# Two-layer hybrid attention network on one core: keys and queries projected ahead of the values, and one pair's keys ahead of the first scores

## The chip, the core and the metric

The kernel runs on one core of a Trainium2 chip. The metric is the device time of one execution in microseconds, the median of several runs. Five engines work side by side, each through its own list of instructions in a fixed order: TensorE (PE in the profile), VectorE (DVE), ScalarE (ACT), GpSimd (POOL) and SyncE (SP), which here only issues DMAs. An instruction that has to wait holds up everything behind it in its engine's list.

## The reference

The network has two layers, 512 tokens, a model width of 1024 and heads of 64. Layer 0 has 8 heads of attention with a decay ("fox"), and 8 heads of attention over the 128 highest-scoring keys of each query ("dsa"), where a small indexer gives the score. Layer 1 has 16 heads of plain causal attention in effect ("moba": with two blocks of 256, the own block and every earlier one are taken). Each layer ends with a gated convolution FFN. Cut to what the change touches:

```python
fq, fk, fv, ff, dq, ckv, dkr, iq, ik, iw = jnp.split(proj, split_points, axis=-1)
log_f = jax.nn.log_sigmoid(ff + b_fox_f)           # decay of each fox head
c = jnp.cumsum(log_f, axis=1)
s = einsum('bqhd,bkhd->bhqk', q_i, k) * scale + c_i - c_k   # fox scores, causal
p = softmax(s); out = einsum('bhqk,bkhd->bqhd', p, v)
score = einsum('bqh,bqhk->bqk', iw, relu(dots)) * idx_scale # indexer, then top_k
```

## The kernel before

All products are float32 made of two parts: each operand is split into a rounded high part (`_h`) and the rest (`_l`), and `mm3` (line 154) multiplies high by high, high by low and low by high. A weight chunk of 128x1024 (`chunk`, line 133) is loaded by SP into `raw`, ACT rounds it to `wh`, and POOL (in the fox and dsa part, where `lo_on_pool` holds) or DVE subtracts to `wl`. `raw`, `wh` and `wl` have three buffers each, so a chunk's `wh` waits until TensorE has done with the chunk three before it.

`proj` (line 160) multiplies one chunk with all tokens: 24 matmuls of 512 columns. A fox pair of heads needs keys (`ks`) and queries (`qs`), one chunk each; every second pair also brings the values of its group of four heads (`vals`, `v_group`, line 385): two chunks, 96 matmuls of 256 columns. Keys and queries are scaled, split and then copied between partitions by DMAs from SP (`stack_k`: six moves, `stack_q`: three), since the scores of the first head of a pair need the two parts of a query stacked.

The order of the program is that of a work list. `heads` (line 524) takes the pairs in turn: first all work numbered up to the pair, then for each of its two heads the scores and the softmax (`soft`), a share of the work of the next pair, and the mix of the head before (`mix`). In layer 0 the index scores of query blocks 1 to 3 (`index_scores`, line 605; names `ix`, `rl`, `tmask`) stand between the pieces of the first pair, and the selections (`select`, line 622) between those of later pairs: 16 rounds of MAX and MATCH_REPLACE on DVE for each block.

A fox score also needs the running sum of the decay, made by a chain of small steps on 32 partitions (lines 641 to 659; names `la`, `lm`, `lu`, `ck`): ACT takes the exponential and the logarithm, each behind a table load, DVE the steps between, ACT and DVE the copies to `ck`. ACT reaches the first relu of the index scores (`rl`) only behind the copies of `ck`.

A scheduler of the framework then sets the order on each engine at build time, from this program order and its own cost table; engines' lists can therefore differ from the order of the source by some instructions.

Of the kernel before, what the change touches and what calls it, by code (L numbers as in the profile page):

```python
# [71 lines left out]
def hybrid_kernel(ctx: ExitStack, tc: tile.TileContext, xT_d, pos_d, const_d, vec_d, w_d, out_d, idx):  # L72
# [60 lines left out]
    def chunk(name, cut=0):  # L133
        raw = wp.tile([P, 1024], F32, tag="raw", bufs=N_W, name=f"raw_{name}")
        wh = wp.tile([P, 1024], F32R, tag="wh", bufs=N_W, name=f"wh_{name}")
        wl = wp.tile([P, 1024], F32R, tag="wl", bufs=N_W, name=f"wl_{name}")
        if cut:
            for s in (slice(0, cut), slice(cut, 1024)):
                nc.sync.dma_start(raw[:, s], w_d[idx[name]][:, s])
                split(wh[:, s], wl[:, s], raw[:, s])  # L140
                if s.start == 0:
                    nc.sync.dma_start(xT[:, 1], xT_d[:, 1])
            return wh, wl
        nc.sync.dma_start(raw, w_d[idx[name]])
        A.copy(wh, raw)  # L145
        if lo_on_pool:
            for n in range(0, 1024, 256):
                t = slice(n, n + 256)
                G.tensor_tensor(wl[:, t], raw[:, t], wh[:, t].bitcast(F32), op=OP.subtract)
        else:  # L150
            V.tensor_tensor(wl, raw, wh.bitcast(F32), op=OP.subtract)
        return wh, wl
# [7 lines left out]
    def proj(name, w=None):  # L160
        wh, wl = w or chunk(name)
        o = ps("mm", f"mm_{name}")
        for k in range(KT):
            s = slice(k * P, k * P + P)
            mm3(o, wh[:, s], wl[:, s], xh[:, k], xl[:, k], k == 0, k == KT - 1)
        return o
# [61 lines left out]
    def scaled(o, nm):  # L228
        y = tmp(f"sc_{nm}")
        V.tensor_tensor(y, o, RB, op=OP.mult)  # L230
        return y
# [11 lines left out]
    def stack_q(y, nm):  # L243

        h, l = halves(y, nm)
        a = big(f"{nm}_a")
        move(a[LO], h[LO])
        move(a[HI], l[LO])
        move(l[LO], h[HI])
        return a, l  # L250

    def stack_k(y, nm, eng=V):

        out = []
        for n, t in zip("hl", halves(y, nm, eng)):
            b = big(f"{nm}_b{n}")
            move(b[LO], t[HI])
            move(b[HI], t[HI])
            move(t[HI], t[LO])
            out += [t, b]  # L260
        return out[0], out[1], out[2], out[3]
# [123 lines left out]
    def v_group(nm, late=None):  # L385

        v = vtile(nm)
        o = [ps("mm", f"mm_{nm}_{b}", (P, 2, 256)) for b in range(2)]
        for c in range(2):
            wh, wl = chunk(f"{nm}{c}")  # L390
            for k in range(4):
                for b in range(NB):
                    s = slice(b * P, b * P + P)
                    kk = 4 * c + k
                    ws = slice(k * 256, k * 256 + 256)
                    mm3(o[b // 2][:, b % 2], xh[:, kk, s], xl[:, kk, s], wh[:, ws], wl[:, ws],
                        kk == 0 and b % 2 == 0, kk == KT - 1 and b % 2 == 1)
            if c == 0 and late is not None:
                late()
        rcol = scale["col"]  # L400
        for b in range(NB):
            src = o[b // 2][:, b % 2].rearrange("p (h c) -> p h c", c=64)
            A.activation(v[:, b, :, 0], src, AF.Identity, scale=rcol[:, b:b + 1])
            V.scalar_tensor_tensor(v[:, b, :, 1], src, rcol[:, b:b + 1], v[:, b, :, 0].bitcast(F32), op0=OP.mult, op1=OP.subtract)
        return v

    def out_proj(nm, o, done=None, part=range(4)):

        for dp in part:
            wh, wl = chunk(f"{nm}{dp}")  # L410
            for e in range(2):
                d = 2 * dp + e
                acc = ps("mm", f"mm_{nm}_{d}")
                for k in range(4):
                    s = slice((4 * e + k) * P, (4 * e + k + 1) * P)
                    mm3(acc, wh[:, s], wl[:, s], o[k][0], o[k][1], k == 0, k == 3)
                V.tensor_tensor(xT[:, d], xT[:, d], acc, op=OP.add)
                if done is not None:
                    done(d)
# [141 lines left out]
    w = chunk("misc", 512)  # L561
# [8 lines left out]
    w = [chunk("iq0")]  # L570
# [34 lines left out]
    def index_scores(i):  # L605
        w = P * (i + 1)
        sc = tmask[i]
        qs = slice(i * P, i * P + P)
        for h in range(4):
            o = ps("S", f"ix{i}_{h}")  # L610
            scores(o[:, :w], iq[h // 2], (ikh, ikh, ikl, ikl), h % 2, qs, w)
            r = tmp(f"rl{i}_{h}")[:, :w]
            wh = iwT[:, i, h:h + 1]
            prev = sc if h else causal[i]
            A.activation(r, o[:, :w], AF.Relu)
            if i == 1:
                V.scalar_tensor_tensor(sc, r, wh, prev, op0=OP.mult, op1=OP.add)
            else:
                A.activation(r, r, AF.Copy, scale=wh)
                G.tensor_tensor(sc, r, prev, op=OP.add)  # L620
# [43 lines left out]
    def fox(p):  # L664
        def vals():
            values["f", p // 2] = v_group(f"fv{p // 2}_")

        def qs():
            c["q"] = stack_q(scaled(proj(f"fq{p}"), f"fq{p}"), f"fq{p}")

        def ks():
            c["k"] = stack_k(scaled(proj(f"fk{p}"), f"fk{p}"), f"fk{p}", G)

        c = {"nm": f"f{p}", "v": ("f", p // 2), "hv": 2 * (p % 2), "bias": causal, "out": fo, "lo": G,
             "decay": [(selr[:, P + h:P + h + 1], ck) for h in (2 * p, 2 * p + 1)]}
        return c, ([vals] if p % 2 == 0 else []) + [ks, qs]

    def dsa(p):
        def vals():
# [29 lines left out]
    pairs, work = [], []  # L709
    for n in range(8):  # L710
        c, w = (fox if n < 4 else dsa)(n % 4)
        pairs.append(c)
        if n == 0:
            w = [x for i, f in enumerate(w) for x in (f, lambda i=i: index_scores(i + 1))]
# [29 lines left out]
    def moba(p):  # L744
        def vals():
            values["m", p // 2] = v_group(f"mv{p // 2}_", moba_scale if p == 0 else None)

        def qs():
            c["q"] = stack_q(rope(proj(f"mq{p}"), f"mq{p}"), f"mq{p}")

        def ks():
            c["k"] = stack_k(rope(proj(f"mk{p}"), f"mk{p}"), f"mk{p}")

        c = {"nm": f"m{p}", "v": ("m", p // 2), "hv": 2 * (p % 2), "bias": causal, "out": mo[p // 4]}
        return c, ([vals] if p % 2 == 0 else []) + [ks, qs]

    pairs, work = [], []
    for n in range(8):
        c, w = moba(n)
        pairs.append(c)  # L760
        work += [(n, f) for f in w]
        if n == 7:
            work.append((7, lambda: out_proj("oo0_", mo[0], part=[0])))
    work += [(8, lambda m=m: out_proj("oo0_", mo[0], part=[m])) for m in range(1, 4)]
# [157 lines left out]
```

## Time and profile before

| | us |
|---|---|
| median of 3 runs | 1264.75 (1263.06 to 1265.96) |
| the profiled execution | 1264.17 |
| its span, first to last instruction | 1262.4 |
| TensorE busy | 1222.1 (97%) |
| VectorE busy | 811.6 (64%) |
| mean granted TensorE clock | 0.995 |

TensorE is busy nearly throughout, so its 40 us of idle time are what a reordering can win, beside what a lower clock costs. Most of it lies in the first 180 us, which hold the start, the fox pairs and the selections. The fox part runs from 44 to about 180 us, dsa and its projection to 265, the first FFN to 640, moba to about 890, and the second FFN to the end.

### The profile page before, as it was taken

How to read it: one execution, taken by the hardware profiler on the slowest of the kernel's cores; microseconds unless marked ns; L12 is line 12 of the kernel's file. 1: busy time of each engine (PE TensorE's matmuls, PEld its weight loads, DVE VectorE, ACT ScalarE, POOL GpSimd, SP SyncE). 2: the span in 40 equal slices, each digit the busy share in tenths (PEclk: the TensorE clock that was granted, in tenths of full speed). 3: DMA queues.
4: the chain of work that ended last, by engine and by line, in shares of the span. 5: the costliest groups of instructions: out<-in, count | busy, mean ns of one | idle time of the engine just before them, and what ended most of it. 6: DMA issues, size and time to landing. Idle time of an engine off the chain costs nothing.

```text
span 1262.4 us, 16801 instructions
## 1 busy us (share of the span) xinstructions
PE 1222.1 (97%) x5996; PEld 1019.0 (81%) x5996; DVE 811.6 (64%) x1489; ACT 557.1 (44%) x969; POOL 359.0 (28%) x394
## 2 busy tenths in 40 slices
PE   6889999999999999999999999999999999999997
PEld 4768777877888888888887888888878888888887
DVE  7889988675554455554666778787655555444555
ACT  5563667654333233333444556556433333332334
POOL 3675557542111111111213223232212111111110
PEclk9999999999999999999999999999999999999998
DMA  5333435122333333333325434332333332333231
GB/s 193 101 100 114 117 101 134 57 82 83 100 100 100 100 94 93 97 90 95 112 93 138 109 106 117 107 107 67 90 95 100 100 94 92 99 100 101 92 92 67
DMA packets 57379, 127.24 MB, mean 101 GB/s; under 512 B 7584, under 2 KB 21024, under 8 KB 57296
## 3 DMA queue, kind: packets, MB, share of 16 engines
q1 hardware_dynamic: 56368, 124.81, 33.5%
q10 hardware_dynamic: 864, 1.17, 0.3%
q8 instruction: 47, 0.77, 0.2%
q14 instruction: 36, 0.29, 0.1%
q0 software_dynamic: 64, 0.20, 0.0%
HBM read 104.13 MB, written 2.10 MB: 84 GB/s over the span
## 4 chain that ended last, share of the span: by engine, by line
PE 75%; DVE 11%; issue 5%; ACT 4%; DMA 2%; POOL 2%; SPq 0%; POOLq 0%; ACTq 0%; DVEq 0%
PE mm_u L157 6%; PE mm_u L156 6%; PE mm_g L157 6%; PE mm_u L158 6%; PE mm_d L157 6%; PE mm_g L158 6%; PE mm_g L156 6%; PE mm_d L158 6%; PE mm_d L156 6%; DVE tmask L627 2%; DVE m L626 1%; PE t_m L369 1%; PE o_m L378 1%; PE mm_mq L157 1%; PE mm_mq L156 1%
## 5 line engine op out<-in xcount | busy, mean ns | idle before, releaser
L431 POOL TENSOR_TENSOR cv<-cv,gs 128x512 f32<-128x512 f32 x44 | 57.1, 1297 | 550.0 <-ACT gs L430 550.0
L156 PE MATMUL mm_d<-a_h,wh_d 128*128 128x512 f32 (+1 forms) x384 | 143.1, 373 | 2.1 <-ACT a_h L128 2.1
L157 PE MATMUL mm_d<-a_l,wh_d 128*128 128x512 f32 (+1 forms) x384 | 142.9, 372 | 0.4 <-DVE a_l L129 0.4
L158 PE MATMUL mm_d<-a_h,wl_d 128*128 128x512 f32 (+1 forms) x384 | 142.7, 372 | 0.0
L500 DVE TENSOR_TENSOR us<-mm_u,cv 128x512 f32<-128x512 f32 x44 | 30.4, 692 | 168.1 <-PE mm_u L158 132.7
L157 PE MATMUL mm_g<-xl,wh_g 128*128 128x512 f32 x352 | 137.2, 390 | 0.4 <-DVE xl L172 0.4
L156 PE MATMUL mm_u<-xh,wh_u 128*128 128x512 f32 x352 | 137.4, 390 | 0.0
L158 PE MATMUL mm_u<-xh,wl_u 128*128 128x512 f32 x352 | 137.1, 389 | 0.0
L157 PE MATMUL mm_u<-xl,wh_u 128*128 128x512 f32 x352 | 137.1, 389 | 0.0
L156 PE MATMUL mm_g<-xh,wh_g 128*128 128x512 f32 x352 | 137.0, 389 | 0.0
L158 PE MATMUL mm_g<-xh,wl_g 128*128 128x512 f32 x352 | 137.0, 389 | 0.0
L145 ACT CAST wh_g<-raw_g 128x1024 fp32r<-128x1024 f32 x44 | 46.3, 1053 | 155.5 <-PE mm_g L157 153.9
L497 DVE TENSOR_TENSOR gs<-mm_g,RB 128x512 f32<-128x512 f32 x44 | 30.4, 691 | 121.9 <-PE mm_g L158 119.5
L128 ACT CAST wh_d<-raw_d 128x1024 fp32r<-128x1024 f32 x45 | 47.4, 1053 | 118.8 <-PE mm_u L157 107.3
L156 PEld LDWEIGHTS mm_d<-a_h,wh_d 128*128 128x128 f32 x384 | 72.4, 188 | 15.5 <-ACT a_h L128 3.0
L157 PEld LDWEIGHTS mm_d<-a_l,wh_d 128*128 128x128 f32 x384 | 72.4, 188 | 13.4 <-DVE a_l L129 1.1
L158 PEld LDWEIGHTS mm_d<-a_h,wl_d 128*128 128x128 f32 x384 | 72.4, 188 | 12.3
L157 PEld LDWEIGHTS mm_g<-xl,wh_g 128*128 128x128 f32 x352 | 66.1, 188 | 14.7 <-DVE xl L172 1.1
L156 PEld LDWEIGHTS mm_g<-xh,wh_g 128*128 128x128 f32 x352 | 66.1, 188 | 13.8
L156 PEld LDWEIGHTS mm_u<-xh,wh_u 128*128 128x128 f32 x352 | 66.1, 188 | 13.7
L158 PEld LDWEIGHTS mm_u<-xh,wl_u 128*128 128x128 f32 x352 | 66.1, 188 | 13.7
L158 PEld LDWEIGHTS mm_g<-xh,wl_g 128*128 128x128 f32 x352 | 66.1, 188 | 13.6
(778 smaller groups left out, 3074.1 us busy)
## 6 DMA issues: line engine op xcount, KB each, us to landing
raw_g<-in_w SPq DMA_DIRECT2D x44, 512.0 KB, 3.5
raw_u<-in_w SPq DMA_DIRECT2D x44, 512.0 KB, 3.6
raw_d<-in_w SPq DMA_DIRECT2D x41, 256.0 KB, 2.9
raw_d<-in_w SPq DMA_DIRECT2D x29, 192.0 KB, 2.6
raw_d<-in_w SPq DMA_DIRECT2D x34, 128.0 KB, 2.6
raw_oe<-in_w SPq DMA_DIRECT2D x8, 512.0 KB, 4.0
raw_mv<-in_w SPq DMA_DIRECT2D x8, 512.0 KB, 3.5
raw_mk<-in_w SPq DMA_DIRECT2D x8, 512.0 KB, 3.7
```

Of the source, the lines that this page charges most:

```text
L128: A.copy(dst_h, src)
L145: A.copy(wh, raw)
L156: PE.matmul(out, ah, bh, start=first, stop=False)
L157: PE.matmul(out, ah, bl, start=False, stop=False)
L158: PE.matmul(out, al, bh, start=False, stop=last)
L369: PE.transpose(t[:, n * P:n * P + P], probs[i][:, j * P:j * P + P], ident)
L378: PE.matmul(o[:, o0:o0 + w], vj, ph[:, c0:c0 + w], start=j == 0, stop=False)
L431: G.tensor_tensor(cv, cv, gs, op=OP.mult)
L497: V.tensor_tensor(gs, og, RB, op=OP.mult)
L500: V.tensor_tensor(us, ou, cv, op=OP.mult)
L626: V.max(m8, sc)
L627: V.match_replace(sc, m8, sc, -3e38)
```

## The change

In layer 0 each fox pair that brings values now projects keys and queries first and the values last. In layer 1 the keys of the second pair get the number of the first, so that they stand in front of the first pair's scores in the work list.

```diff
-        return c, ([vals] if p % 2 == 0 else []) + [ks, qs]
+        return c, [ks, qs] + ([vals] if p % 2 == 0 else [])
...
     for n in range(8):
         c, w = moba(n)
         pairs.append(c)
-        work += [(n, f) for f in w]
+
+        work += [(0 if n == 1 and f is w[0] else n, f) for f in w]
```

The index scores of the first pair keep their places in the list, one behind each piece: block 1 now comes behind the keys instead of the values, block 2 behind the queries, block 3 behind the values. Taken in order, the first four chunks after `ckv` were fv, fv, fk, fq and are now fk, fq, fv, fv.

On ACT, the stretch around the exponential and the logarithm of the decay (`la`, `lu`), with `ckv_h` the high part of the normalized latent keys, - before and + now:

```order
 L633 ACTIVATE sqkv<-sc_ckv 128x512
 L643 ACTIVATE la<-ry_misc,vec 32x512
+L145 CAST wh_fv_1_687<-raw_fv_1_686 128x1024
+L128 CAST ckv_h<-ckvn 128x512
 L645 ACT_TABLE_LOAD
 L645 ACTIVATE la<-la 32x512
-L128 CAST ckv_h<-ckvn 128x512
-L145 CAST wh_fq_708<-raw_fq_707 128x1024
 L648 ACT_TABLE_LOAD
 L648 ACTIVATE lu<-lu 32x512
```

The rounding of the fourth chunk moved from behind the exponential to in front of its table load; the chunk three before it is now fk.

On DVE, where the first fox scores (`s_f_0`, `s_f_1`) are read between the selection rounds of block 1 (`m_1_1306` is the first round, each next one is numbered 3 higher). Before:

```order
L627 MATCH_REPLACE tmask_91<-m_1_1345,tmask_91 128x256
L626 MAX m_1_1348<-tmask_91 128x8
L345 ISA prt_f_781,mx_f_0_786<-s_f_0_782,cmask 128x128
L345 ISA mx_f_0_786 128x1
L345 ISA prt_f_781,mx_f_1_793<-s_f_1_789,cmask 128x256
```

Now:

```order
L627 MATCH_REPLACE tmask_91<-m_1_1336,tmask_91 128x256
L345 ISA prt_f_781,mx_f_0_786<-s_f_0_782,cmask 128x128
L345 ISA mx_f_0_786 128x1
L626 MAX m_1_1339<-tmask_91 128x8
L345 ISA prt_f_781,mx_f_1_793<-s_f_1_789,cmask 128x256
```

Eleven rounds stand in front of the first score now, fourteen and a MAX did before.

On TensorE in layer 1, from the second head's third scores (`s_m_2` with `mk_bh`) through the transposes of the first head's probabilities (`t_m`). Before:

```order
L265 MATMUL s_m_2_6021<-mk_bh,mq_l 128x384
L266 MATMUL s_m_2_6021<-mk_bl,mq_l 128x384
L265 MATMUL s_m_3_6027<-mk_bh,mq_l 128x512
L266 MATMUL s_m_3_6027<-mk_bl,mq_l 128x512
L369 MATMUL t_m_0_6088<-const,prt_m_5928 128x128 x2
L369 MATMUL t_m_1_6095<-const,prt_m_5928 128x128
```

Now:

```order
L265 MATMUL s_m_2_6066<-mk_bh,mq_l 128x384
L266 MATMUL s_m_2_6066<-mk_bl,mq_l 128x384
L369 MATMUL t_m_0_6088<-const,prt_m_5977 128x128 x3
L369 MATMUL t_m_1_6095<-const,prt_m_5977 128x128 x2
L369 MATMUL t_m_0_6088<-const,prt_m_5977 128x128
L265 MATMUL s_m_3_6072<-mk_bh,mq_l 128x512
L266 MATMUL s_m_3_6072<-mk_bl,mq_l 128x512
L369 MATMUL t_m_1_6095<-const,prt_m_5977 128x128
```

The last scores moved behind most of the transposes. Ahead of this place the list is as before up to the fourth scores of the first head: the 24 matmuls of the second pair's keys and 15 of its queries already stood in front of the first score, and SP's list of loads and moves is the same row for row.

## Rows read from the trace of the kernel before

**Rows 1.** Waits of TensorE from 40 to 200 us.

```profile
engine line waited for: us in total, times, longest us
PE s_f L265 <- DMA fq_a<-fq_l: 2.7, 1, 2.7
PE t_f L369 <- DVE pt_f_0l L129: 2.2, 4, 1.3
```

**Rows 2.** Windows: busy time of each engine by stretch.

```profile
core 0: us, PE busy (x) PEld busy (x) DVE busy (x) ACT busy (x) POOL busy (x), PEclk, DMA share, GB/s
...
85.00:90.00 5.00, 5.00 (x21) 4.35 (x21) 3.58 (x14) 3.52 (x10) 1.04 (x2) 0.66 0.12 26
90.00:165.00 75.00, 72.73 (x422) 62.09 (x422) 71.77 (x192) 40.23 (x96) 42.76 (x63) 1.00 0.43 115
```

**Rows 3.** Timeline of TensorE: start, duration, instruction, [idle before, what ended it].

```profile
33.07 0.62 PE L201 MATMUL bc_n<-const,y_n 128*128 128x128 f32 x4 [2.23 <-DVE y_n L198]
...
44.02 0.28 PE L156 MATMUL mm_fv__0_483<-wh_fv,xh 128*128 128x256 f32 x1
...
51.25 0.62 PE L201 MATMUL bc_kv<-const,y_kv 128*128 128x128 f32 x4 [0.56 <-DVE y_kv L198]
...
58.78 0.40 PE L156 MATMUL mm_fk<-xh,wh_fk 128*128 128x512 f32 x1
...
62.21 0.39 PE L156 MATMUL mm_fk<-xh,wh_fk 128*128 128x512 f32 x1
...
64.20 0.38 PE L265 MATMUL ix<-ik_h,iq_a 128*128 128x256 f32 x1 [1.60 <-ACT rl L615]
...
84.61 0.39 PE L265 MATMUL s_f<-fk_h,fq_a 128*128 128x256 f32 x1 [2.72 <-DMA fq_a<-fq_l]
...
168.03 0.50 PE L156 MATMUL mm_dq<-xh,wh_dq 128*128 128x512 f32 x1 [1.76 <-DVE dv L129]
```

**Rows 4.** Timeline of DVE: decay chain, a selection round, first fox scores.

```profile
51.91 0.75 DVE L636 SCALAR_TENSOR_TENSOR ckvn<-sc_ckv,vec,bc_kv 128x512 f32<-128x512 f32 x1 [0.81 <-PE bc_kv L201]
...
53.55 0.69 DVE L647 SCALAR_TENSOR_TENSOR la<-lu,la 32x512 f32<-32x512 f32 x1
...
56.23 1.28 DVE L649 TENSOR_TENSOR lm<-lm,lu 32x512 f32<-32x512 f32 x1 [1.27 <-ACT lu L648]
57.55 1.12 DVE L650 TENSOR_TENSOR lm<-lm,la 32x512 f32<-32x512 f32 x1
...
62.90 1.70 DVE L659 CAST ck<-ckt 32x512 fp32r<-32x512 f32 x2
...
69.15 0.43 DVE L626 MAX8 m<-tmask 128x8 f32<-128x256 f32 x1
...
70.14 0.43 DVE L626 MAX8 m<-tmask 128x8 f32<-128x256 f32 x1
...
85.15 0.29 DVE L345 CUSTOM_DVE_ANT_0 prt_f<-s_f,cmask 128x128 f32<-128x128 f32 x1 [1.81 <-PE s_f L266]
...
87.22 0.56 DVE L345 CUSTOM_DVE_ANT_0 prt_f<-s_f,cmask 128x384 f32<-128x384 f32 x1 [0.52 <-PE s_f L266]
...
88.50 0.69 DVE L345 CUSTOM_DVE_ANT_0 prt_f<-s_f,cmask 128x512 f32<-128x512 f32 x1 [0.71 <-PE s_f L266]
```

**Rows 5.** Timeline of ACT around the decay's exponential and logarithm.

```profile
52.69 0.62 ACT L128 CAST ckv_h<-ckvn 128x512 fp32r<-128x512 f32 x1 [2.90 <-DVE ckvn L636]
53.22 1.05 ACT L145 CAST wh_fq<-raw_fq 128x1024 fp32r<-128x1024 f32 x1
54.28 1.28 ACT L648 ACT_TABLE_LOAD   x1
55.57 0.63 ACT L648 ACTIVATE lu<-lu 32x512 f32<-32x512 f32 x1
```

**Rows 6.** Timeline of POOL at the same time.

```profile
54.39 3.72 POOL L149 TENSOR_TENSOR wl_fq<-raw_fq,wh_fq 128x256 fp32r<-128x256 f32 x4 [5.49 <-issue]
```

**Rows 7.** The chain that ended last: the second move of the queries.

```profile
80.31 4.26 DMA fq_a<-fq_l
```

**Rows 8.** Timeline of TensorE in layer 1, at the first probabilities.

```profile
680.46 0.44 PE L369 MATMUL t_m<-const,prt_m 128*128 128x128 f32 x2 [1.48 <-POOL prt_m L350]
```

## The prediction

> **What bounds the kernel now.** I read the waits of TensorE first. In the fox part one wait leads: 2.7 us of the first scores for the move of the queries [rows 1]. The timeline shows it as a gap ahead of 84.61, and an earlier one of 1.60 ahead of the third index score, which waits for ACT's relu [rows 3]. Then the windows: from 85 to 90 us the granted clock averages 0.66, that is about 3.4 us at 1.2 GHz after that gap, where the same matmuls take twice as long; this costs about 1.7 us. From 90 to 165 us both engines are full: TensorE 72.7 of 75 us, DVE 71.8 [rows 2]. DVE holds up TensorE there, four times for 2.2 us [rows 1] and for 1.76 at 168 [rows 3]. So a start won on TensorE before 90 us is kept only as far as DVE gets its list done earlier as well. After 180 us TensorE runs almost without gaps, and what is won or lost by then goes straight into the end.
>
> DVE has 3.05 us of idle time ahead of 90, waiting for fox scores: 1.81, 0.52 and 0.71 [rows 4]. This is the stock from which the change can pay on DVE; 1.27 more lie in the decay chain, waiting for the logarithm.
>
> **The change in layer 0, step by step.** No arithmetic is added or removed; every price is one of order.
>
> *Chunks.* fk and fq now take the first two places. A chunk of either kind is the same load of 512 KB, and 24 matmuls at 0.229 us (16 starts from 58.78 to 62.21 [rows 3]) last 5.5 us; 48 of half the columns, at an estimated half of that, the same. The beat of loads, roundings and POOL subtractions stays, so no price for those: they hide under a chunk's 5.5 us, and would cost their 1.05 us on ACT each if they did not.
>
> *The moves.* Nine DMAs are issued per pair on SP. With keys and queries done by about 58 us on TensorE, fk's parts wait for ACT (below) until about 65.5 and fq's until about 69; the last move that the first head needs lands about 4.3 us after its issue [rows 7], so by about 74. The loads ahead of the moves in SP's list wait for POOL's subtraction of the fifth chunk, at about 64, as early as the moves are ready. TensorE has the values (96 matmuls, 11 us), twelve index scores and 14 matmuls of the next keys between fq and the first fox scores, and reaches these at about 79. The 2.72 us wait goes. What is late next is DVE.
>
> *The decay chain on ACT.* Here the change costs. The rounding of the fourth chunk now stands ahead of `ckv_h` and of the exponential's table load, and must wait until TensorE has done with fk. TensorE starts it at 44.02, loses its place to the latent norm until 51.25 + 0.62 [rows 3] and has two matmuls left, so ACT starts that rounding at about 52.2 and ends at 53.25. Then `ckv_h` 0.6, table load 1.28, exponential 0.63, table load 1.28 and logarithm 0.63 (sizes of [rows 5]) end at about 57.65. Before, the exponential lay in ACT's idle time of 2.90 ahead of `ckv_h`, and the logarithm ended at 55.57 + 0.63 = 56.2 [rows 5]. The chain is 1.45 us late.
>
> DVE goes on from there. With the steps as long as before, the last copy of `ck` ends 1.45 later than its 62.90 + 1.70 = 64.6 [rows 4]. It then has two value copies fewer behind it (0.9 us) and one scaling more (0.6): 1.8 us late in equal work. But the steps on `lm` may shrink: 1.28 and 1.12 while POOL subtracts a chunk until 58.1 [rows 6], against 0.69 for a step of the same shape with POOL idle [rows 4]. POOL starts that subtraction behind the rounding, so it would now end at about 57 (53.25 + 3.72), before the steps come: that gives back 1.0. The Trainium skill has a rule for it (SBUF — State Buffer, Who interferes with whom): a DVE instruction with two inputs in SBUF and a POOL instruction that reads SBUF exclude each other. By the rule the loss on DVE is 0.8, by rows repeated as they are 1.8; the rows here agree with it. I take the middle, 1.3, with both ends for the range.
>
> *First fox scores.* DVE reached the end of its work ahead of the first score at 85.15 - 1.81 = 83.3, that is 18.7 us behind `ck`. Now three rounds and a MAX fewer stand there; a round is 0.99, from 69.15 to 70.14 [rows 4], so 3.4 us. With two value copies more and a scaling less it is 15.6 us, and DVE is there at about 80.7 to 81.7. TensorE, at 79, can make two scores; the third needs the buffer of the first and waits until 81 to 82. So TensorE waits 1.2 to 2.3 us here, but DVE does not: its idle 3.05 us are gone. DVE gains 3.05 - 1.3 = **1.7 us** (1.25 to 2.25).
>
> *The wait for the relu.* The third index score now stands behind fq and 37 matmuls of the values, at about 62.5 us, where it stood before; the relu comes behind `ck`, at 63.3 to 64.6 instead of 63.76. It stays a wait of 0.8 to 2.0 us, off DVE's path, so 0.
>
> *Later pairs.* In the second group keys and queries also come first, so that values instead of projections fill the place of the next pair's mix. Both engines are full there before and after, at the same work; a new DVE idle costs at most about one wait as seen there (1.3, the longest of [rows 1]), and a lost one of 1.76 ahead of 168 would gain that. I take 0, with -1.8 and +1.3 for the range.
>
> **The change in layer 1.** The build had the second pair's keys ahead of the first scores already, so the stated edit moves nothing there. What moves is the second head's last scores, behind the transposes. These wait 1.48 us for POOL's normalization [rows 8]. Four more matmuls of 256 columns (0.5) fill that wait now, but the scores of 512 columns (2 x 0.23) leave it: 0. The second head's softmax gets later by some 3.5 us; it is needed only after 96 value matmuls and a projection, about 17 us further, which cover it; without that cover it would cost the 3.5.
>
> **Sum.** 1264.17 of the profiled execution (span 1262.4 and 1.8 around it) less 1.7 is 1262.5. The median of the runs is 0.6 above that execution, so I forecast 1264.75 - 1.7 = **1263.0**. A measurement of this kernel tells about 0.2% (2.5 us) from no change, so this counts as the same.
>
> **The rivals.**
> First, *the new wait takes what the old one gave.* TensorE still idles 1.2 to 2.3 us ahead of the third score. Idle stretches of 2.23 (ahead of 33.07) and 2.72 were followed by 1.2 GHz, that of 1.76 ahead of 168 was not [rows 3]. If the clock falls, the scores take twice as long, 1.7 us in all, and DVE waits for them after all: 0, 1264.7. The Trainium skill (TensorE: Matmul & The Clock Gate, Part 1) says that the gate's watch is not tied to the kernel's own start; by that the same idle may or may not meet a fall, and these three rows can't decide it.
>
> Second, *TensorE's waits were what counted.* If the engines are less bound to each other than the windows look, the gaps go in full: 2.72, the clock's 1.7, and DVE's whole idle (3.05 and, with contention gone, 1.27 in the chain and 0.81 ahead of it [rows 4]) allows 5.1: 1259.6. For it speaks that TensorE's wait on DVE from 90 to 165 is only 2.2 us; against it that DVE has 3.2 us of slack in 75.
>
> Third, *slower: the late decay chain.* Its price falls at the relu wait and the third score. If the chain is 1.8 late, both waits reach 2.0 to 2.3, and the clock falls at both and once more at the transposes where TensorE waits for DVE: 3 x 1.7 = 5.1 in place of the one fall of 1.7, DVE 1.8 late less 3.05: +2.2, **1266.9**. It decides from an idle stretch of between 1.76 and 2.23.
>
> Fourth, *the change doesn't do what it says* in layer 1, which the order already shows; in layer 0 the builder's list has it.
>
> **How the numbers follow.** Forecast 0.42; first rival 0.22; second 0.22; third 0.14. Faster by over 0.2% (under 1262.2) are the second rival and nearly a third of the forecast, whose own range, 1260.5 to 1265, reaches below: 0.34. Slower by over 0.2% (above 1267.3) is the half of the third rival and a little: 0.10. Same: 0.56. The range takes in the second rival's 1259.6 with some of its spread and nearly all of the third: 1259.0 to 1266.8.
>
> **What would show it.** In the profile after, the gap ahead of the first `s_f` scores for a DMA is gone, and the third `s_f` scores wait for DVE instead; the logarithm on ACT ends at about 57.7; the clock between 80 and 90 us stays full (forecast) or not (first and third rival); DVE's idle at the first fox scores, 3.05 before, is gone; and dsa's first projections, at 168.03 before, start about 1.7 earlier. From there on the kernel should run as before. I am wrong if the fox part gives more than 3 us or loses any, or if layer 1 moves by more than half a microsecond.

## The result and the profile after

The changed kernel takes 1274.25 us (median of 4 runs, 1271.79 to 1275.26) against 1264.51 for the kernel before in the same set: a ratio of 1.0068, 95% interval 1.0052 to 1.0084. That is slower by 8.6 us by the ratio and by 9.7 by the two medians; 1263.0 was forecast, with 1266.8 as the upper end.

The profiled execution grew by 9.7 us, from a span of 1262.4 to 1272.1. The page of the kernel after says in its head:

```profile
span 1272.1 us, 16797 instructions
PE 1224.1 (96%) x5996; PEld 1019.9 (80%) x5996; DVE 813.2 (64%) x1489; ACT 557.4 (44%) x969; POOL 359.1 (28%) x394
```

TensorE is busy 2.0 us longer than before (1222.1) with the same 5996 instructions, as stretches at a lower clock would make it; it idles 7.7 us more. The waits of TensorE from 40 to 200 us of the kernel after, to be laid beside [rows 1]:

```profile
engine line waited for: us in total, times, longest us
PE s_f L265 <- DMA fq_a<-fq_h: 4.9, 2, 2.9
PE t_f L369 <- DVE pt_f_0l L129: 3.4, 2, 2.2
PE ix L265 <- ACT rl L615: 3.4, 2, 1.9
PE s_d L265 <- DMA dq_a<-dq_l: 1.8, 1, 1.8
PE mm_dq L156 <- DVE dv L129: 1.8, 1, 1.8
```

The 2.7 us for the move of the queries is not gone: it has become 4.9 in two places, and there is one more of 1.8 at dsa. In all, TensorE's waits in this stretch grew from 10.7 to 17.4 us: the moves are half of that (3.5), the rest is more waiting for the relu (1.4), for DVE's part of the transposes (1.2) and small ones. TensorE's timeline of the kernel after tells where:

```profile
80.01 0.28 PE L265 MATMUL s_f<-fk_h,fq_a 128*128 128x256 f32 x1
...
102.48 0.35 PE L265 MATMUL s_f<-fk_h,fq_a 128*128 128x256 f32 x1 [1.92 <-DMA fq_a<-fq_h]
...
118.81 0.55 PE L369 MATMUL t_f<-const,prt_f 128*128 128x128 f32 x3 [2.25 <-DVE pt_f_0l L129]
...
162.97 0.36 PE L265 MATMUL s_f<-fk_h,fq_a 128*128 128x256 f32 x1 [2.93 <-DMA fq_a<-fq_h]
...
172.81 0.50 PE L156 MATMUL mm_dq<-xh,wh_dq 128*128 128x512 f32 x1 [1.81 <-DVE dv L129]
...
181.22 0.36 PE L265 MATMUL s_d<-dk_h,dq_a 128*128 128x256 f32 x1 [1.83 <-DMA dq_a<-dq_l]
```

The first scores start at 80.01 without a wait, against 84.61 with 2.72 [rows 3]; that is what the change was forecast to do. Not all of the 4.6 us is the order's. DVE's step on `ckvn` stands ahead of what the change moves on DVE and started at 51.91 before [rows 4]; in this execution it starts 1.4 us earlier (DVE's timeline of the kernel after):

```profile
50.53 0.75 DVE L636 SCALAR_TENSOR_TENSOR ckvn<-sc_ckv,vec,bc_kv 128x512 f32<-128x512 f32 x1 [0.81 <-PE bc_kv L201]
```

In all 18 traces of this case it starts between 50.5 and 52.05, so a shift of up to 1.5 us can be there before the order matters. The second pair's scores (102.48), the fourth's (162.97) and dsa's first (181.22) now wait. DVE waits with TensorE, here at the second pair (3.54 us at the fourth), as its timeline of the kernel after shows:

```profile
103.11 0.29 DVE L345 CUSTOM_DVE_ANT_0 prt_f<-s_f,cmask 128x128 f32<-128x128 f32 x1 [2.06 <-PE s_f L266]
```

Three stretches at the lower clock stand behind waits, and the windows of the kernel after catch each of them (the first reaches back into 100 to 105, with 0.82):

```profile
core 0: us, PE busy (x) PEld busy (x) DVE busy (x) ACT busy (x) POOL busy (x), PEclk, DMA share, GB/s
...
85.00:90.00 5.00, 5.00 (x26) 4.26 (x26) 4.97 (x21) 3.80 (x10) 4.73 (x8) 1.00 0.23 52
90.00:165.00 75.00, 66.70 (x372) 56.78 (x371) 65.20 (x167) 34.37 (x80) 37.39 (x54) 0.95 0.39 103
...
105.00:110.00 5.00, 5.00 (x20) 4.05 (x19) 4.19 (x12) 3.27 (x8) 1.82 (x3) 0.84 0.00 0
...
120.00:125.00 5.00, 5.00 (x26) 4.71 (x27) 3.76 (x12) 3.47 (x10) 0.41 (x1) 0.66 0.36 133
...
180.00:185.00 5.00, 3.78 (x12) 3.15 (x13) 1.87 (x5) 2.52 (x6) 3.32 (x5) 0.67 0.36 82
```

From 85 to 90 the clock is full, where it averaged 0.66 before; from 90 to 165 TensorE is busy 66.7 us and DVE 65.2, where they were busy 72.7 and 71.8 [rows 2].

A ruler for all runs is the moment at which DVE reads the first score of a head. Its shift against the kernel before, in us, from DVE's timelines of the profiled executions (before, in absolute time, in the first row):

| kernel | fox 1 | fox 3 | fox 5 | fox 7 | dsa 1 | dsa 8 |
|---|---|---|---|---|---|---|
| before | 85.15 | 102.64 | 138.06 | 158.57 | 179.55 | 240.14 |
| after | -4.31 | +0.47 | -0.77 | +5.02 | +6.50 | +9.67 |

The gain is there at the first head and spent at the third. From dsa's fourth head on the shift stays between 9.64 and 9.67, and at the end of layer 1 the last `y_n` is 9.5 late. **All of the loss arises between 85 and 204 us, in layer 0; layer 1 adds nothing.**

**Why the moves are late.** SP's timeline of the kernel after, at the second and the fourth pair (`raw_fq` and `raw_oe` are loads of weight chunks, `fq_a` the moves of the queries):

```profile
96.72 0.34 SPq L144 DMA_DIRECT2D raw_fq<-in_w  x1
97.10 0.46 SPq L241 DMA_DIRECT2D fq_a<-fq_h  x1
...
157.40 0.33 SPq L144 DMA_DIRECT2D raw_oe<-in_w  x1
157.83 0.46 SPq L241 DMA_DIRECT2D fq_a<-fq_h  x1
```

The kernel before had them in the other order at the second pair (SP's timeline):

```profile
98.70 0.55 SPq L241 DMA_DIRECT2D fq_a<-fq_h  x1
99.38 0.51 SPq L241 DMA_DIRECT2D fq_a<-fq_l  x1
100.51 0.34 SPq L144 DMA_DIRECT2D raw_fq<-in_w  x1
```

At the fourth pair the load stood in front of the moves before, too, but 1.8 us ahead of the first of them, and no wait followed (SP's timeline of the kernel before):

```profile
151.82 0.33 SPq L144 DMA_DIRECT2D raw_oe<-in_w  x1
...
153.64 0.46 SPq L241 DMA_DIRECT2D fq_a<-fq_h  x1
```

So there the order is as it was and only the time changed: the load waits for POOL's subtraction `wl_dq`, which ended at 151.80 before and ends at 157.38 in the kernel after.

What the load of the second pair waits for, by POOL's timeline of the kernel after, and behind it DVE's, with the step that makes the moved data:

```profile
93.42 3.27 POOL L149 TENSOR_TENSOR wl_fv<-raw_fv,wh_fv 128x256 fp32r<-128x256 f32 x4
```

```profile
94.84 1.26 DVE L129 TENSOR_TENSOR fq_l<-sc_fq,fq_h 128x512 fp32r<-128x512 f32 x1
```

A load of 512 KB needs a raw buffer, which is free when POOL's subtraction ends (96.69). The load goes out 0.03 us later, the moves behind it, though `fq_l` was done at 96.1. And they don't only go late, they land late. The moves behind that load, and those of the next pair with nothing in front (columns: out<-in, queue, operation, count, KB, us from issue to landing; kernel after):

```profile
raw_fq<-in_w SPq DMA_DIRECT2D x1, 512.0 KB, 4.6
fq_a<-fq_h SPq DMA_DIRECT2D x1, 128.0 KB, 4.7
fq_a<-fq_l SPq DMA_DIRECT2D x1, 128.0 KB, 4.8
...
fq_a<-fq_h SPq DMA_DIRECT2D x1, 128.0 KB, 2.3
fq_a<-fq_l SPq DMA_DIRECT2D x1, 128.0 KB, 2.2
```

Wherever the load went out within a microsecond ahead of them, the moves took 4.1 to 5.0 us (before: first fox pair and first dsa pair; after: second, fourth and first dsa pair); free ones took 2.2 to 2.3. With the load further ahead they land sooner: 3.5 us behind one 1.1 us ahead (third pair of the kernel before), 2.5 behind the one 1.8 us ahead. The 4.26 of [rows 7] was such a blocked one. The Trainium skill (DMA: Bandwidth & Descriptors, Queues, rings and completion order) says that descriptors on a DMA engine are consumed in ring order; the trace agrees with 2.3 against 4.7 us for the same 128 KB. No run here separates that order from the load's bytes simply taking the engines' time.

### The profile page after: what moved, and what is told of

It reads as the page before. It is cut to its first block, busy times and chain, and to the rows that moved or that the text cites. A ratio compares the mean times of both kernels' runs of the same rounds, so it can differ in the third digit from the quotient of the medians.

```text
span 1272.1 us, 16797 instructions
## 1 busy us (share of the span) xinstructions
PE 1224.1 (96%) x5996; PEld 1019.9 (80%) x5996; DVE 813.2 (64%) x1489; ACT 557.4 (44%) x969; POOL 359.1 (28%) x394
## 4 chain that ended last, share of the span: by engine, by line
PE 72%; issue 5%; DVE 4%; ACT 3%; POOL 2%; DMA 2%; POOLq 0%; ACTq 0%; SPq 0%; DVEq 0%
PE mm_u L156 6%; PE mm_u L157 6%; PE mm_g L157 6%; PE mm_u L158 6%; PE mm_d L157 6%; PE mm_g L156 6%; PE mm_g L158 6%; PE mm_d L158 6%; PE mm_d L156 5%; PE t_m L369 1%; PE o_m L378 1%; PE mm_mk L157 1%; PE mm_mk L156 1%; PE mm_mk L158 1%; PE mm_mq L157 1%
```

## The experiments

**Which part costs?** Three kernels carry one part each: layer 1 with layer 0's line as before (e1), the first group of layer 0 (e2, first line below in place of before's), or the second (e3, second line); e2 and e3 have layer 1 as before.

```diff
-        return c, ([vals] if p % 2 == 0 else []) + [ks, qs]
+        return c, [ks, qs, vals] if p == 0 else [vals, ks, qs] if p == 2 else [ks, qs]
...
+        return c, [vals, ks, qs] if p == 0 else [ks, qs, vals] if p == 2 else [ks, qs]
```

> The layer-1 edit alone; layer 0 as in the kernel before. In the trace of the changed kernel everything after 204 us is shifted by the same 9.65 us, so both theories put the whole loss into layer 0: ratio to before 1.000 within 0.0010, 1263.5 to 1265.8 us. The rival that some of the loss sits in layer 1 needs a ratio over 1.002 (over 1267).

Measured: 1265.61 us, ratio 0.9993 (0.9983 to 1.0002). Layer 1 is worth nothing, as the prediction had it.

> Only the first fox pair has its values last; the third pair and layer 1 as before. Queue theory: the move of the second pair's queries stands behind a chunk load here too, so the 4.3 us won at the first scores are lost again at the third head; the later heads are as before: 1263 to 1267. Theory of TensorE's lead (values late leave no filler): the first group loses its own share of some 4.5 us and the clock falls: also 1264 to 1267. If the first group alone brings most of the loss, the time is above 1270.

> Only the third fox pair has its values last; the first pair and layer 1 as before. The second pair's move stands free of a load here, as in before. If the loss of 5.4 us at the seventh head comes from the order of the second group by itself: 1268 to 1272. If it comes from TensorE's lead having been used up earlier (two falls of the clock at 103 and 120 us), the second group alone costs little: 1264 to 1267.

Measured: 1275.12, 1.0070 (1.0046 to 1.0094), and 1276.98, 1.0079 (1.0055 to 1.0104). Both lie above what the theories expected, 1267 at most for e2, with over 1270 as the sign that the first group brings most of the loss, and 1272 at most for e3. Each half costs as much as both, so the parts don't add. Each order sets anew which load stands in front of which moves: in e2 `raw_fq` ahead of the second pair's and `raw_dq` ahead of the third pair's (2.97 us of wait at 139.33); in e3 the first pair keeps its wait (2.87 at 84.23) and the fourth has one (2.69 at 159.53).

**Loads behind the moves.** If that is the cause, a load queued behind the move it stood in front of must give the time back. The edit only changes SP's order (`issue_after` queues an instruction on its engine behind the named one and adds no wait):

```diff
+    sent, BEHIND = {}, {"fq3": "fq1", "oe0_0": "fq3", "oe0_1": "dq0"}
...
-        nc.sync.dma_start(raw, w_d[idx[name]])
+        with tc.issue_after(sent[BEHIND[name]]) if name in BEHIND else nullcontext(): nc.sync.dma_start(raw, w_d[idx[name]])
...
-        move(a[HI], l[LO])
+        sent[nm] = move(a[HI], l[LO]).ins
```

> The changed kernel with three chunk loads queued behind the second move of the queries (second fox pair, fourth fox pair, first dsa pair) in place of in front. Queue theory: the moves are issued as soon as their halves are ready and land after 2.2 to 2.4 us instead of 4.5 to 5.0; the waits of 1.92, 2.93 and 1.83 us shrink below 0.5 each, and the falls of the clock behind the first and third go: 1263 to 1267. Theory of TensorE's lead: waits of the same size turn up under other names (DVE, POOL), 1271 to 1274. In between, 1267 to 1271: the queue is one cause and the clock or DVE another.

Measured: 1268.61, 1.0020 (1.0011 to 1.0029). By the ratios, 6.1 of the 8.6 us come back (0.0048 of 1265), give or take 2.3. The time lies in the class between the two theories, where the queue is one cause and something else another. TensorE's waits for `fq_a` are gone, and what leads them from 40 to 205 us is now `mm_dq`, waiting for DVE's `dv` twice, 2.35 and 2.65 us. The cause of the second stands in three timelines of e4, first POOL's, then DVE's, then TensorE's:

```profile
194.75 2.15 POOL L149 TENSOR_TENSOR wl_oe<-raw_oe,wh_oe 128x256 fp32r<-128x256 f32 x3 [4.39 <-ACT wh_oe L145]
196.85 1.27 POOL L224 TENSOR_TENSOR rs_dq<-rs_dq,SR 128x512 f32<-128x512 f32 x1
```

```profile
198.16 1.19 DVE L225 TENSOR_TENSOR ry_dq<-ry_dq,rs_dq 128x512 f32<-128x512 f32 x1 [2.73 <-POOL rs_dq L224]
199.36 0.66 DVE L129 TENSOR_TENSOR dv<-mm_dv,dv 128x512 fp32r<-128x512 f32 x1
```

```profile
200.07 0.50 PE L156 MATMUL mm_dq<-xh,wh_dq 128*128 128x512 f32 x1 [2.65 <-DVE dv L129]
```

It is the same pattern on POOL: prefetch work (`wl_oe`, needed much later) ahead of the rope product that DVE waits for; behind DVE's waiting sum stands the evacuation of `dv`, and TensorE waits for that. The next kernel is e4 with this subtraction behind the product:

```diff
-    sent, BEHIND = {}, {"fq3": "fq1", "oe0_0": "fq3", "oe0_1": "dq0"}
+    sent, BEHIND = {}, {"fq3": "fq1", "oe0_0": "fq3", "oe0_1": "dq0", "wl_oe0_0": "rs_dq2"}
...
-        G.tensor_tensor(s, s, SR, op=OP.mult)
+        sent["rs_" + nm] = G.tensor_tensor(s, s, SR, op=OP.mult).ins
...
-                G.tensor_tensor(wl[:, t], raw[:, t], wh[:, t].bitcast(F32), op=OP.subtract)
+                with tc.issue_after(sent[BEHIND["wl_" + name]]) if "wl_" + name in BEHIND else nullcontext(): G.tensor_tensor(wl[:, t], raw[:, t], wh[:, t].bitcast(F32), op=OP.subtract)
```

> As the run before with the loads behind the moves, and one more edit: on POOL the rope product of the third dsa pair stands ahead of the subtraction of the first output-projection chunk. In the earlier run's trace DVE waits 2.73 us for that product at 198 us with the evacuation of the dsa values queued behind it, TensorE waits 2.65 us for the evacuation and then runs at 1.2 GHz for some 5 us. If this queue on POOL is what gives the gain back: 4 to 5 us faster than that run, 1262 to 1265. If the loss there is TensorE's lead being spent, whatever the name of the wait: within 1.5 us of that run, 1267 to 1269.

Measured: 1264.56, 0.9984 (0.9975 to 0.9994). Another 4.6 us come back, give or take 1.7; the product starts at 194.93 and TensorE waits 0.77 in place of 2.65 (POOL's and TensorE's timelines of e5):

```profile
194.93 1.30 POOL L224 TENSOR_TENSOR rs_dq<-rs_dq,SR 128x512 f32<-128x512 f32 x1 [4.58 <-DVE rs_dq L222]
```

```profile
198.19 0.50 PE L156 MATMUL mm_dq<-xh,wh_dq 128*128 128x512 f32 x1 [0.77 <-DVE dv L129]
```

This is not a second part of what the change lost, and 6.1 and 4.6 are not to be added: together they are more than the 8.6. The wait arises only in e4. In the kernel before the subtraction stands ahead of the product as well (194.78 and 197.56), and in the kernel after it is over before the product's input is there, so that the product waits for DVE and not for POOL's list (POOL's timeline of the kernel after):

```profile
202.77 2.81 POOL L149 TENSOR_TENSOR wl_oe<-raw_oe,wh_oe 128x256 fp32r<-128x256 f32 x4
206.25 1.29 POOL L224 TENSOR_TENSOR rs_dq<-rs_dq,SR 128x512 f32<-128x512 f32 x1 [0.67 <-DVE rs_dq L222]
```

Neither kernel has a wait of TensorE for `mm_dq` there. It seems to be the time won ahead of this place that makes the subtraction and the product meet in e4, and e5 keeps that gain.

Two kernels take one entry of e4's table each, `{"fq3": "fq1"}` (second pair) and `{"oe0_0": "fq3"}` (fourth):

> The changed kernel with only the load of the fourth pair's query chunk queued behind the second pair's moves. Queue theory: the wait of 1.92 us at the third head and the fall of the clock behind it go, the place at the seventh head stays: 2 to 4 us less than the changed kernel, 1269.5 to 1272.5. If the places are not independent (the gain is lost again at the seventh head because its moves wait for POOL until the same time): 1273 to 1275.

> The changed kernel with only the first output-projection load queued behind the fourth pair's moves. Queue theory: the wait of 2.93 us at the seventh head shrinks below 0.7, nothing changes before: 2.5 to 5 us less than the changed kernel, 1268.5 to 1272. Theory of TensorE's lead: the wait returns under another name, 1273 to 1275.

Measured: 1271.77, 1.0040 (1.0024 to 1.0055), and 1272.38, 1.0042 (1.0023 to 1.0061): 3.5 and 3.3 us given back by the ratios, with some 3 us of uncertainty on each, so both are only just clear of noise (and e7 lies 0.4 above its expected range). That is near what each wait cost, 1.92 and the 1.7 of the 1.2 GHz stretch behind it at the second pair, 2.93 at the fourth, but the agreement is loose: in e6's trace dsa's first head is 7.8 us earlier than in the kernel after, its eighth only 3.0.

**The same cure on the old order.** The kernel before has blocked moves too: its first pair (the wait of [rows 1]) and dsa's first. e8 is the kernel before with `{"fq2": "fq0", "fq3": "fq1", "oe0_0": "fq3", "oe0_1": "dq0", "wl_oe0_0": "rs_dq2"}`, e9 adds `{"oe0_2": "dq1", "oe0_3": "dq2"}`, and e10 is the changed kernel with e9's table but for `fq2`, where nothing stands in front.

> The kernel before, in its own order of projections, with all four loads behind the moves and the rope product ahead on POOL. Queue theory: its one wait of this kind, 2.72 us at the first scores, shrinks by the 2 us that the move lands sooner, and the fall of the clock behind it may go: 1.5 to 4 us faster than before, 1261 to 1263.5. If the moves' place is only harmful with the values last, no change: 1264 to 1266.

> The order of the kernel before; all of its query moves in layer 0 ahead of the chunk loads (two more dsa places than in the run before), rope product ahead on POOL. In the earlier run's trace the two further moves still stand behind a load; TensorE waits 0.83 us for the one at 202 us and some 2 us are lost between the third and the fifth dsa head. Queue theory: 1 to 2.5 us faster than that run, 1259.5 to 1262. If these places are covered: the same, 1261.5 to 1263.

> The changed order in both fox groups, otherwise as the first kernel of this set. Queue theory: what is left of the change's loss without the queue is the order's own worth, forecast in the prediction as a gain of 1.7; against the first kernel of the set between -2 and +1.5: 1259 to 1263. If the values last cost TensorE its filler at the same time: 2 to 4 us slower than the first kernel of the set.

Measured: e8 1262.10, 0.9969 (0.9947 to 0.9992); e9 1260.44, 0.9974 (0.9960 to 0.9988); e10 1262.56, 0.9986 (0.9976 to 0.9996). e8 and e9 can't be told apart. So the wait that the change was made against (2.7 us for `fq_a`, gone from TensorE's waits in e8) goes just as well without the change, by the order of entries on SP. How much of the time e8's exchange on POOL brings was not separated. The changed order with free moves is no better than the old one with free moves.

**Each half again, moves free.** e11 and e12 are e2 and e3 with e10's table (e12 with `"fv1_1": "fq0"` besides). e13 is e11 and `"dq2": "fq2"`, since e11 still has a load in front of the third pair's moves, as its traces showed; e14 is e9 and the same entry.

> Only the first group reordered, all moves free. In traces so far the first group's order brings 3.3 to 4.3 us at the first scores against the kernel before, but only 0 to 1 against the kernel before with free moves, and a late decay chain costs 1.5 on the relu waits: 1260 to 1264, within 1.5 us of the first kernel of the set.

> Only the second group reordered, all moves free. Queue theory: within 2 us of the first kernel of the set, where the same order with loads ahead cost 10 us: 1260 to 1264. If the second group's order by itself starves the seventh head: 1266 or more.

Measured: 1269.59, 1.0039 (1.0025 to 1.0053), and 1267.86, 1.0024 (1.0010 to 1.0038). In e11 the cause is in plain sight, in SP's and in TensorE's timeline:

```profile
131.80 0.33 SPq L144 DMA_DIRECT2D raw_dq<-in_w  x1
132.22 0.46 SPq L241 DMA_DIRECT2D fq_a<-fq_h  x1
```

```profile
137.15 0.39 PE L265 MATMUL s_f<-fk_h,fq_a 128*128 128x256 f32 x1 [1.78 <-DMA fq_a<-fq_l]
```

Both times miss the expected 1260 to 1264; e12's lies in the range of the rival that the second group's order by itself starves the seventh head. e12's runs spread from 1263.19 to 1272.65, and its profile is the shortest of them, where TensorE waits only 0.5 us for `fq_a`; why the others are longer stays open, beyond a lower mean clock in their lists (0.993 on average).

> As the run with only the first group reordered and its moves free, and one more load (a dsa query chunk) behind the third pair's moves, where that run still had it in front: its trace shows a wait of 1.79 us for that move at 137 us, and its lead over the kernel before falls from 4.2 to 0.4 us there. Queue theory: 2.5 to 5 us faster than that run, 1264.5 to 1267. If the first group's order costs by itself, whatever stands in the queue: within 1.5 us of it, 1268 to 1271.

> The fastest run so far (the order of the kernel before, its moves free) with the third pair's moves freed as well. There the load stood in front too, but no wait followed it in the trace: queue theory and any other: 1259.5 to 1261.5, within 1 us of that run; a gain of more than 2 us would say that a move hidden behind other work matters as well.

Measured: e13 1265.82, 1.0004 (0.9993 to 1.0015): one load more behind a move is worth 0.35%, 4.4 us (give or take 2.3), and the wait of 1.78 is gone (the move of `fq_l` lands after 2.4 us, in e11 after 4.4). e14 1259.47, 0.9960 (0.9945 to 0.9975): **the old order with seven loads behind the moves and the one subtraction behind the rope product beats both kernels**, the one before by 5.1 us. How that divides between the loads and the exchange on POOL was not tried, and the intervals of e14 and e9 overlap, as expected. TensorE's waits from 40 to 200 us of e14 no longer have the moves of `fq_a` among them; this one leads now:

```profile
PE t_f L369 <- DVE pt_f_0l L129: 2.8, 4, 1.0
```

With free moves each half still costs more than the old order: e13 is 0.0044 above e14 (5.6 us) and e12 0.0050 above e9 (6.3 us), while both halves together (e10) lie much nearer. So the moves are not all of what a half costs. In e13 POOL's list has, ahead of dsa's first projections, the place that is shown below for e10, and TensorE waits 2.35 us there (ahead of 166.18); exchanging it in e13 was not tried.

**What parts the two orders still?** e10 lies 2 us above e9. One theory was the late decay chain of the prediction's sum; e15 is e10 with the rounding of the fourth chunk behind the logarithm:

```diff
-    A.activation(lu[R], lu[R], AF.Ln)
+    sent["ln"] = A.activation(lu[R], lu[R], AF.Ln).ins
...
-        A.copy(wh, raw)
+        with tc.issue_after(sent["ln"]) if name == "fv0_1" else nullcontext(): A.copy(wh, raw)
```

> The changed order with all moves free, and on ACT the rounding of the fourth chunk behind the logarithm of the decay, so that the exponential and ckv_h stand as in the kernel before. If the late decay chain is what makes the changed order slower than the old one with free moves (two relu waits of 1.5 and 1.96 us against 1.59 and 0.4): 1 to 2 us faster, 1260.5 to 1262. If that wait is off the path, as the prediction had it: 1262 to 1263.5.

Measured: 1266.10, 1.0004 (0.9991 to 1.0017), slower than e10, which neither theory expected. The chain is earlier (logarithm at 54.24 in place of the kernel after's 55.99), but the rounding stands later, and the two relu waits, 1.46 and 1.94 in the kernel after, become one, with a long stretch of low clock behind it (TensorE's timeline of e15, then its windows):

```profile
78.44 0.80 PE L265 MATMUL ix<-ik_h,iq_a 128*128 128x512 f32 x1 [3.07 <-ACT rl L615]
```

```profile
75.00:80.00 5.00, 1.93 (x6) 1.28 (x5) 4.83 (x17) 3.05 (x7) 2.38 (x4) 0.74 0.59 203
80.00:85.00 5.00, 5.00 (x19) 4.23 (x17) 2.79 (x11) 4.17 (x8) 4.69 (x4) 0.57 0.00 0
```

So an earlier logarithm by this edit buys nothing. It does not clear the chain, though: the same edit makes the later relu wait. The traces of e10 and e9 differ most at 165 us: in e10 POOL's normalization of the seventh head's probabilities stands ahead of dsa's first rope product, in e9 behind it. e10's timelines of POOL and of TensorE:

```profile
159.28 2.06 POOL L350 TENSOR_SCALAR prt_f<-prt_f,sm_f 128x128 f32<-128x128 f32 x4 [5.29 <-DVE sm_f L348]
161.29 1.29 POOL L224 TENSOR_TENSOR rs_dq<-rs_dq,SR 128x512 f32<-128x512 f32 x1
```

```profile
165.13 0.50 PE L156 MATMUL mm_dq<-xh,wh_dq 128*128 128x512 f32 x1 [2.33 <-DVE dv L129]
```

e16 is e10 with these two exchanged (the head's normalization is written where its probabilities are used, so that the product is known by then); all other engines keep their lists row for row.

```diff
-            G.tensor_scalar(neg, neg, sm[:, i:i + 1], 1.0, op0=OP.mult, op1=OP.mult)
+            with tc.issue_after(sent["rs_dq0"]) if nm == "f30" else nullcontext(): G.tensor_scalar(neg, neg, sm[:, i:i + 1], 1.0, op0=OP.mult, op1=OP.mult)
```

> The changed kernel with all of its moves free (1262.56), and one thing more: the normalization of the seventh fox head's probabilities on POOL (four instructions, 2.06 us at 159.28) stands behind the rope product of dsa's first projection (1.29 at 161.29) and not ahead of it; the other four engines' lists are the same row for row. In the old order with the same free moves (1260.44) the product stands in front already: there DVE's sum of the rope does not wait, dv is evacuated 0.29 us late for TensorE, and no stretch at 1.2 GHz follows; here DVE waits 1.67, TensorE 2.33 ahead of 165.13, and the clock averages 0.66 from 165 to 170 us. Theory, that POOL's order at this one place is what still parts the two orders: the 2.33 shrinks to 0.3 to 1.0 (0.7 us of a subtraction still stand ahead), the 1.2 GHz stretch behind it goes (1.7), first score of dsa's first head 2.5 to 4 us earlier, time 1258.5 to 1260.5, ratio 0.995 to 0.997. Rival, that what parts them is spread over the run (the decay chain, the relu waits): the wait goes but comes back at the transposes of the seventh head, whose probabilities are now normalized 1.3 us or more later, and the time stays at 1262 to 1263, ratio 0.998 to 0.999.

Measured: 1261.64, 0.9974 (0.9962 to 0.9986). The time is 1.1 above the theory's range and 0.4 below the rival's; as a ratio it is e9's. In TensorE's timeline of e16 the wait has halved, and the clock behind it is full (165 to 170 us: 1.00, in e10 0.66):

```profile
163.24 0.50 PE L157 MATMUL mm_dq<-xh,wh_dq 128*128 128x512 f32 x1 [1.25 <-DVE dv L129]
```

It did not come back at the seventh head's transposes. e10's profile is its longest run (1265.90), so its 1.2 GHz stretch there need not be in its other runs; the gain of 0.9 us between the medians (1.5 by the ratios, give or take 2.0) fits the shorter wait alone. The intervals of e10 and e16 overlap, so this place is likely, and not proven, to be what parted the two orders.

One limit holds for most of these: where a load is queued elsewhere on SP, the build also places instructions of other engines anew. In e4 some 250 places of DVE's list differ, and DVE reads the third head's first score behind 22 selection rounds, in the kernel after behind 23. So the 6.1 us of e4 are what the loads behind the moves bring together with the order that the build makes of it. Only e16 against e10 (POOL) and e14 against e9 (SP) differ in one engine's list alone, and e5 against e4 leaves TensorE's and SP's lists as they are; e14 and e9 can't be told apart. That late moves make the waits is shown by the traces; that they make all of the lost time is not.

## Why the prediction was wrong, step by step

**Right.** *First fox scores*: the 2.72 us wait went, the scores are read 4.3 us earlier (80.84), without idle time on DVE. Of the 4.3 the early start of this execution is 1.4; counted from `ckvn`, DVE needed 30.3 us, where the forecast's 80.7 to 81.7 allows 28.8 to 29.8, so that 80.84 lies in it by luck. *DVE's gain of 1.7*: at the third head DVE runs out of work at 101.05, 1.4 us earlier than before, with one selection round more done (1.25); less the early start that is 1.3 us won, the low end of 1.25 to 2.25. *The decay chain*: the logarithm starts at 55.99 and ends 0.42 later than before, though everything ahead of it ran 1.4 us earlier in this execution: 1.8 late against 1.45 forecast. *POOL's contention*: the steps on `lm` took 0.69 and 0.69 in place of 1.28 and 1.12 [rows 4], though the one on `la` ahead of them now met POOL and took 1.11 in place of 0.69. DVE's timeline of the kernel after:

```profile
54.85 1.11 DVE L647 SCALAR_TENSOR_TENSOR la<-lu,la 32x512 f32<-32x512 f32 x1
...
56.65 0.69 DVE L649 TENSOR_TENSOR lm<-lm,lu 32x512 f32<-32x512 f32 x1 [0.69 <-ACT lu L648]
```

*Layer 1*: 0. *Full clock from 80 to 90*: so it came; the wait at the third score was 0.2 where 1.2 to 2.3 was forecast.

**Wrong: the step "Later pairs".** It took 0, with -1.8 to +1.3 for the range, from the busy shares of [rows 2], and put no SP list behind it: no price stood there for a move that gets late. Only the first pair's nine moves were walked past their loads. The built order already showed `raw_fq` in front of the second pair's `fq_a`; the first `raw_oe` stood in front of the fourth's in both kernels, so there the times had to be worked out, with the load waiting for POOL. The rows for a price were there: [rows 7] has a move of 4.26 us behind a load, and free moves of 2.3 stood in the same trace. An estimate made with the result known, two pairs waiting 2 to 3 us each and two stretches at 1.2 GHz of 1.7 (the prediction's own figure), gives 7.4 to 9.4 us. It is near what came partly by luck: no fall came behind the fourth pair's wait.

What the runs show in place of the 0: -1.7 was forecast for the span and +9.7 came, so the term measured +11.4 (10.3 by the ratio of the runs; 12.4 in this pair of executions if the early start and DVE's gain of 1.3 are counted). The waits for late moves are part of it, 1.92 ahead of 102.48, 2.93 ahead of 162.97 and 1.83 ahead of 181.22, and freeing these moves gives 6.1 us back (e4, give or take 2.3). The other 4 or so are not taken apart by any run. They come back where all moves are free and the exchange on POOL is in: e10 lies 0.0014, or 1.8 us, under the kernel before, which is the forecast's 1.7 by size, but the old order with the same freedom lies lower still. What a half of the changed order costs beside its moves (e12, e13) stays open too.

**Wrong: that DVE's gain lasts.** The prediction said itself that TensorE's start is kept only where DVE gets its list done earlier. DVE did, by 1.3 us and the early start, and lost it at 103.11, where it waited 2.06 us for the next blocked pair. A gain ahead of the next wait is no gain if a third engine sets that wait's end: here `raw_fq`, and the moves behind it, waited for POOL's subtraction.

**dsa's first projections** were to start 1.7 earlier than 168.03 [rows 3]; they started 4.8 later, which was the plainest sign named beforehand.

**The rivals.** The third had three stretches at 1.2 GHz, and three came, but at 103, 120 and 182 us, behind blocked moves and the transposes, and not at the relu waits of the decay chain: these were 1.46 and 1.94 us, and the clock is 1.00 in the windows from 60 to 100 us of the kernel after. Its point of decision, an idle stretch between 1.76 and 2.23 us, does not hold: in the kernel after 1.92 ahead of 102.48 and 1.83 ahead of 181.22 were followed by a fall, and 2.93 ahead of 162.97 was not. The 2.23 ahead of 33.07 fell before [rows 3]; the same idle after did not. The Trainium skill (TensorE: Matmul & The Clock Gate, Part 1) says that the gate's watch is not tied to the kernel's start; this last pair agrees with it. The range failed because no rival was about the moves of the later pairs; its upper end came from the wrong mechanism.

## What to carry to other kernels

Where a change renumbers a work list, walk the in-order list of every queue that it feeds, to the last pair, and look for a prefetch (a load that waits for a buffer, a rounding, a subtraction) that now stands in front of something a busy engine waits for. A load can stand in front in both versions and do harm in one only, so look at the times too. A small move right behind a large load on the same queue pays twice: for the load's own wait, and by landing with it. Queue such loads behind the moves by hand first, and only then judge an order of the work; here that was worth 5 us on the old order, together with one exchange on POOL, and the new order bought nothing beyond it. And compare two traces from a place ahead of the change: one execution can be ahead of another by a microsecond from the start.

## What the hardware did that was not expected

A 128 KB move lands 2.2 to 2.3 us after its issue with nothing in front and 4.1 to 5.0 when a 512 KB load was issued within a microsecond before it. The load itself took 4.6, and the move landed about half a microsecond after it; with the load 1.1 us ahead it was 3.5.

Which idle of TensorE a lower clock follows can't be told here from its length: 1.83 and 1.92 us were followed by 1.2 GHz, 2.93 was not, in one execution.

Runs of one program differ in the mean granted clock listed with them, and the time goes with it: over some hundred runs of the kernel before, in the sets of all experiments, the mean time is 1263.1 us at a clock of 0.997, 1265.6 at 0.994 and 1267.8 at 0.992, some 0.8 to 0.9 us for each 0.001. A difference of 2 us between kernels can come from that alone; at a dozen runs each, the intervals of e9, e10 and e16 still overlap.
